# The first product's bank copied into a second bank of PSUM, and the second product accumulated there

## The chip, the cores and the metric

The kernel runs on one core of a Trainium2 chip. The metric is the device time of one execution, in microseconds. The engines are TensorE (PE in the profile; its weight loads are PEld), VectorE (DVE), ScalarE (ACT), GpSimd (POOL) and SyncE (SP). SP and POOL issue most DMAs here.

## The reference

One encoder layer on two sequences, a sample of 1024 tokens and a prompt of 512, with width 2048, in float32. What matters of it:

```python
h = rms_norm(x, norm_g)
z = h @ w_in                                   # 2048 -> 5632 columns
c_val, c_glu, c_gate, q, k, v, a_gate = jnp.split(z, split_points, axis=-1)
...                                            # rope on q and k
conv_out = conformer_conv(c_val, c_glu, ...) * jax.nn.silu(c_gate)   # 31 taps, layer norm, silu, @ w_pw
attn_out = banded_sink_attention(q, k, v, sink) * jax.nn.silu(a_gate)
mix = jnp.concatenate([conv_out, attn_out], axis=-1) @ w_out
return rms_norm(x + mix, final_norm_g)
```

## The kernel before

Every large product is made of matmuls of 128x128 weights against 512 tokens. For accuracy an operand is split into a high and a low part of a rounded format (`parts`, line 506: a ScalarE copy for the high part, a VectorE subtraction for the low one), and three matmuls stand for one: high by high, high by low, low by high.

The sample's input projection is written as *units* (class `Unit`). A unit multiplies two column tiles of the weights by two halves of the tokens over two groups of four row tiles. That is a product of 2x2 block matrices, and it is done in Winograd's form with seven block products instead of eight: P1, P2, P6, P5, P7, P3, P4 (the order `ALONE`, one name per step). Each is 4 x 3 = 12 matmuls, 84 for a unit. `SUMS` says which sum of tokens a product streams, `OPERAND` which split weight tile (`hl`, four per unit, made by `make0` to `make3`) it reads, `BANK` which of the unit's three PSUM banks it goes to. Products named in `FRESH` begin a bank, the others accumulate on what stands in it.

After each product `tap` takes the bank away. A ScalarE copy (line 236) goes to a buffer of the pools u or g, four buffers each, which are handed out in turn by `E()`. Where a partial result needs two banks, a VectorE addition follows (line 257). So the first result is: P1 copied, then P2's bank added to the copy; the bank of P1 goes on collecting P6, P7 and P4. `finish` hands a result on: in the first and third stage POOL's queue stores it (line 268), in the second and fourth a DMA of POOL's queue adds the stored half to it (line 501), and after four further steps (`landing`) its follow-up runs: gates, rope, silu.

The weights: `load0` and `load1` fetch two raw tiles of 512 KB by SP's queue into three buffers, `make0` splits the first, `make1` subtracts (three VectorE operations, line 143), then splits the sums, `less2` and `make2` follow on the second tile, `make3` on the last sum. There are three `hl` buffers; a product that is the last to read one gives it back, and `w_prep` is called in each product to make the next ones. A `Prep` says how many loads ahead are to be issued after it (`lead`).

The order of stages: a first plain unit, then seven units (first half of the rows, convolution columns), eight (second half of the same), fourteen (first half, the other columns) and fourteen (second half). At the head of the first, second and fourth the units run as a pair, product by product in turn. `switch` prepares the sums of tokens for the next stage in the last unit of the first and third. Beside the units, lanes of small work run by credit: the convolution's taps on VectorE, sums and norms, attention. After the units come the prompt's jobs, the pointwise products, the output projection in units of class `Onto`, and the last products for the prompt.

The Tile framework orders the instructions of each engine by priority and by its own reckoning of when each can begin, and sets the semaphores. `high_priority` moves an instruction ahead, `issue_after` behind another of the same engine. On the chip each engine takes its instructions in that order.

Of the kernel before, what the change touches and what calls it, by code (L numbers as in the profile page):

```python
# [57 lines left out]
ALONE = ("P1", "P2", "P6", "P5", "P7", "P3", "P4")  # L58
DIRECT = ("P1", "P2", "P3")
ENDS = (ALONE, ("P1", "P2", "P6", "P5", "P7", "P3", "P4"))  # L60
TURNS = ("P1", "P2", "P5", "P6", "P7", "P3", "P4")


# [30 lines left out]
class Unit:  # L94
# [10 lines left out]
    def __init__(self, e, w, cols, k, part, done=None, keep=None):  # L105
        self.e, self.k, self.part, self.done, self.keep = e, k, part, done, keep
        self.total = done is not None
        self.w = [w[c][:, k : k + 2 * HALF, :] for c in cols]
        self.before, self.after, self.d = [], {}, {}
        self.side = False  # L110
        self.order = ALONE
        self.sums = None


    def preps(self):
        return [Prep(load, make, 3) for load, make in ((self.load0, self.make0), (self.load1, self.make1), (None, self.make2), (None, self.make3))]

    def raw(self):
        return self.side([2, HALF, P], F32) if self.side else self.e.raw_tile()

    def load0(self):
        self.r1 = self.e.raw_tile()
# [12 lines left out]
    def make0(self):  # L135
        t = self.e.hl_tile()
        self.e.parts(t[:, 0], t[:, 1], self.r1)
        if self.keep:
            self.e.store(self.keep[0][:, self.k : self.k + 2 * HALF, :], t[:, 1].bitcast(F32).rearrange("p a b c -> p (a b) c"))
        return t  # L140

    def sub(self, out, x, y):
        self.e.nc.vector.tensor_tensor(out, x, y, ALU.subtract)

    def make1(self):

        if self.late:
            t2 = self.e.G([HALF, P]) if self.side or not self.total else self.e.A([HALF, P], F32)
        else:
            t2 = self.e.PT("p", NP, [HALF, P])  # L150
        r1, r2 = self.r1, self.r2
        self.sub(r1[:, 0], r2[:, 0], r1[:, 0])
        self.sub(t2, r2[:, 1], r1[:, 0])
        self.sub(r1[:, 1], r1[:, 1], t2)
        if self.sums:
            for name, x in (("P5", r1[:, 0]), ("P6", t2), ("P4", r1[:, 1])):
                self.e.store(self.sums[name], x)
        t = self.e.hl_tile()
        for o, x in enumerate((r1[:, 0], t2)):
            self.e.parts(t[:, 0, o], t[:, 1, o], x)  # L160
        return t

    def less2(self):
# [29 lines left out]
    def product(self, step, late):  # L193
# [4 lines left out]
        e.w_prep(i + 1)  # L198
        hl = e.hl[i]
        n = BANK[name]  # L200
        if name in FRESH:
            self.bank[n] = e.PS(self.tags[n], [W])
        acc = self.bank[n]
        toks = e.T[SUMS[name]]
        for j in range(HALF):
            for q, (l, r) in enumerate(((0, 0), (0, 1), (1, 0))):
                nc.tensor.matmul(  # L207
                    acc,
                    hl[:, l, o, j, :],
                    toks[j][:, r],  # L210
                    start=name in FRESH and j == 0 and q == 0,
                    stop=name in LAST and j == HALF - 1 and q == 2,
                    skip_group_check=True,
                )
            if j == 0:
                for fn in late:
                    fn()
                if step or not self.alone:
                    e.w_prep(i + self.look)
                else:  # L220
                    e.lessen(self)
                e.turn_over()
            e.tick(3 * MM)
        if step in (1, 3, 5, 6):
            e.hl.pop(i)
        for fn in self.after.get(step, ()):
            fn()
# [2 lines left out]
    def tap(self, name):  # L230

        e, nc = self.e, self.e.nc
        bank = self.bank[BANK[name]]
        if name not in ("P2", "P3"):
            t = e.E()
            nc.scalar.activation(t, bank, AF.Copy)  # L236
            self.copied = nc.cur_bb.bb.instructions[-1]
# [12 lines left out]
        elif name == "P3":  # L250
            self.add((0, 1), bank)
        else:
            self.d[1, 0] = t
            self.finish((1, 0))

    def add(self, n, x):
        self.e.nc.vector.tensor_tensor(self.d[n], x, self.d[n], ALU.add)
# [13 lines left out]
class Onto(Unit):  # L271
# [5 lines left out]

    def __init__(self, e, w, cols, k, source, part, done=None):
        super().__init__(e, w, cols, k, part, done)
        self.source, self.next, self.ahead = source, None, 2  # L280

    def begin(self, n):
# [96 lines left out]
class Prep:  # L379


    def __init__(self, load, make, lead=2, behind=False):
        self.load, self.make, self.lead, self.behind = load, make, lead, behind


class Job:
# [44 lines left out]
class Encoder:  # L431
# [199 lines left out]

    def w_prep_now(self, upto):
        while self.ready < min(upto, len(self.preps)):
            self.w_load(self.ready + 1)
            prep = self.preps[self.ready]
            with self.behind() if prep.behind else ExitStack():
                self.hl[self.ready] = prep.make()
            self.ready += 1
# [1236 lines left out]
def encoder(ctx, tc, a):  # L1875
# [18 lines left out]
    def grouped(units, two):  # L1894
        if not two:
            return [[u] for u in units]
        units[1].side = two
        return [units[:2]] + [[u] for u in units[2:]]

    items = [grouped(units, room) for units, room in zip([stages[0][1:]] + stages[1:], (e.A, e.F, None, e.F))]  # L1900
# [48 lines left out]
    def switch(unit, nxt, g, seq):  # L1949

        held = {}

        roomy = seq is sample

        def load(step):
            held[step] = seq.load_sum(SUMS[ALONE[step]], g, step % 3 or roomy and step == 6)

        def follow(step):
            for j, x in enumerate(held.pop(step)):
                seq.token_sum(SUMS[ALONE[step]], g, j, x)  # L1960
            if step < 4 - roomy:
                load(step + 3)
            elif step == 4 and roomy:
# [214 lines left out]
```

## Time and profile before

| | |
|---|---|
| median of three runs | 2076.07 us (2073.94 to 2077.29) |
| the profiled execution | 2079.13 us, span 2077.4 us |
| mean granted TensorE clock | 0.998 |
| PE busy | 2060.1 us, 9256 matmuls |
| VectorE busy | 1728.4 us |
| ScalarE busy | 1081.8 us |
| POOL busy | 157.9 us |
| HBM | 237 GB/s over the span |

The span runs from the first to the last instruction of one execution. Busy times are per engine and overlap. A row of the timeline has the start, the length, the engine, the line of the kernel, the operation with what it writes and reads, the count, and in brackets how long the engine stood idle before it and what ended that. A merged row of matmuls reaches from the first one's start to the last one's modelled end.

### The profile page before, as it was taken

The numbers are of one execution on the slowest core, as the hardware profiler recorded it, in microseconds if no ns is written. First come the engines' busy times: TensorE is split into PE (matmuls) and PEld (weight loads), VectorE is DVE, ScalarE is ACT, GpSimd is POOL, SyncE is SP. The second block draws the span as 40 slices with busy tenths as digits, with TensorE's granted clock in tenths as the row PEclk, the third lists the DMA queues.
The fourth block names the chain that finished last, engine by engine and source line by source line (L and its number), as shares of the span: only waits on it lengthen the run. The fifth ranks groups of instructions, "written<-read, shape, count | busy, mean of one in ns | idle before, by whom it ended". The sixth has DMA issues, their size and how long they took to land.

```text
span 2077.4 us, 27223 instructions
## 1 busy us (share of the span) xinstructions
PE 2060.1 (99%) x9256; PEld 1697.9 (82%) x9256; DVE 1728.4 (83%) x2843; ACT 1081.8 (52%) x1771; POOL 157.9 (8%) x240
## 2 busy tenths in 40 slices
PE   9999999999999999999999999999999999999998
PEld 8888888888888888788888888888888887888886
DVE  8768899998899899889766777776799978998877
ACT  7486445333465555655555777336553343454454
POOL 0111111111112111100000000000000111100000
PEclk9999999999999999999999999999999999999999
DMA  8888886864577777954555555997789898778897
GB/s 285 309 300 256 200 215 226 286 218 158 190 243 197 181 167 179 279 167 158 164 183 185 178 172 188 316 329 233 239 295 295 279 324 283 213 259 277 293 324 279
DMA packets 242300, 494.56 MB, mean 238 GB/s; under 512 B 23664, under 2 KB 84464, under 8 KB 242160
## 3 DMA queue, kind: packets, MB, share of 16 engines
q1 hardware_dynamic: 216352, 428.83, 62.1%
q0 software_dynamic: 24512, 61.88, 12.5%
q10 hardware_dynamic: 1296, 2.11, 0.3%
q8 instruction: 72, 1.18, 0.2%
q14 instruction: 68, 0.56, 0.1%
HBM read 331.77 MB, written 160.96 MB: 237 GB/s over the span
## 4 chain that ended last, share of the span: by engine, by line
PE 73%; issue 8%; DMA 8%; DVE 7%; ACT 2%; POOL 1%; SPq 0%; ACTq 0%; POOLq 0%; DVEq 0%
PE a L207 21%; PE a L670 13%; PE c L207 10%; PE b L670 6%; PE c L670 6%; PE b L207 5%; PE s L1169 2%; PE pv L1198 2%; PE a L1852 2%; PE s L207 2%; DVE hl L511 2%; PE pt L1203 1%; PE s L1852 1%; DVE t L511 1%; DMA p<-y_d 1%
## 5 line engine op out<-in xcount | busy, mean ns | idle before, releaser
L207 PE MATMUL a<-t,hl 128*128 128x512 f32 x2640 | 632.5, 390 | 1.8 <-ACT u L236 1.3
L207 PEld LDWEIGHTS a<-t,hl 128*128 128x128 f32 x2640 | 493.5, 188 | 108.4 <-ACT u L236 2.4
L511 DVE TENSOR_TENSOR hl<-raw,hl 128x1024 fp32r<-128x1024 f32 (+3 forms) x334 | 337.8, 1012 | 151.5 <-ACT hl L510 147.3
L510 ACT ACTIVATE hl<-raw 128x1024 fp32r<-128x1024 f32 (+3 forms) x334 | 296.8, 889 | 314.4 <-PE c L207 88.1
L670 PE MATMUL a<-t,hl 128*128 128x512 f32 x1344 | 326.3, 393 | 0.0
L207 PE MATMUL c<-t,hl 128*128 128x512 f32 x1320 | 319.1, 389 | 0.0
L670 PEld LDWEIGHTS a<-t,hl 128*128 128x128 f32 x1344 | 248.8, 188 | 50.4
L207 PEld LDWEIGHTS c<-t,hl 128*128 128x128 f32 x1320 | 247.4, 188 | 51.5 <-DVE u L304 0.2
L1041 DVE SCALAR_TENSOR_TENSOR f<-f,c_w_dw,f 128x512 f32<-128x512 f32 x248 | 172.9, 744 | 0.2
L670 PE MATMUL b<-t,hl 128*128 128x512 f32 x672 | 162.9, 392 | 1.5 <-DVE t L515 0.8
L670 PE MATMUL c<-t,hl 128*128 128x512 f32 x672 | 163.9, 393 | 0.0
L1004 DVE SCALAR_TENSOR_TENSOR f<-f,c_w_dw,f 128x512 f32<-128x512 f32 x232 | 163.4, 742 | 0.2
L207 PE MATMUL b<-t,hl 128*128 128x512 f32 x660 | 159.8, 389 | 0.0
L670 PEld LDWEIGHTS b<-t,hl 128*128 128x128 f32 x672 | 124.8, 188 | 27.5 <-DVE t L515 1.1
L670 PEld LDWEIGHTS c<-t,hl 128*128 128x128 f32 x672 | 124.6, 188 | 24.8
L207 PEld LDWEIGHTS b<-t,hl 128*128 128x128 f32 x660 | 123.7, 188 | 25.6
L1033 DVE SCALAR_TENSOR_TENSOR f<-f,w_both,f 128x512 f32<-128x512 f32 x120 | 89.8, 748 | 2.0
L236 ACT ACTIVATE u<-a 128x512 f32<-128x512 f32 x82 | 48.8, 595 | 77.3 <-PE a L207 70.6
L236 ACT ACTIVATE g<-a 128x512 f32<-128x512 f32 x78 | 46.5, 596 | 78.5 <-PE a L207 68.5
L1183 ACT ACTIVATE p<-p,tiny 128x384 f32<-128x384 f32 (+1 forms) x96 | 54.6, 570 | 45.9 <-DVE tiny L1180 36.2
L510 ACT ACTIVATE a<-pt 128x512 fp32r<-128x512 f32 x64 | 38.0, 593 | 64.6 <-PE pt L1203 64.4
L285 POOL DMA_DIRECT2D g<-xT_s x16 | 8.8, 551 | 743.1 <-DMA att_d<-u 669.0
(356 smaller groups left out, 2765.2 us busy)
## 6 DMA issues: line engine op xcount, KB each, us to landing
raw<-w_in SPq DMA_DIRECT2D x170, 512.0 KB, 5.2
raw<-w_out SPq DMA_DIRECT2D x31, 512.0 KB, 5.1
raw<-w_pw SPq DMA_DIRECT2D x24, 512.0 KB, 4.2
wsum_P<-raw SPq DMA_DIRECT2D x47, 256.0 KB, 3.6
raw<-wsum_P SPq DMA_DIRECT2D x18, 512.0 KB, 5.1
f<-x_s SPq DMA_DIRECT2D x16, 512.0 KB, 8.5
g<-wsum_P SPq DMA_DIRECT2D x28, 256.0 KB, 4.6
a<-sum_S SPq DMA_DIRECT2D x24, 256.0 KB, 6.1
```

Source lines behind the costliest of these rows:

```text
L207: nc.tensor.matmul(acc, hl[:, l, o, j, :], toks[j][:, r], start=name in FRESH and j == 0 and q == 0, stop=name in LAST and j == HALF - 1 a ...
L236: nc.scalar.activation(t, bank, AF.Copy)
L510: nc.scalar.activation(hi, x, AF.Copy)
L511: nc.vector.tensor_tensor(lo, x, hi.bitcast(F32), ALU.subtract)
L670: nc.tensor.matmul(job.acc[0], hl[:, l, kk // HALF, kk % HALF, :], r, start=i == 0 and p == 0, stop=i == nk - 1 and p == 2,)
L1004: nc.vector.scalar_tensor_tensor(t, h[:, j : j + T], w(j), t, ALU.mult, ALU.add)
L1033: nc.vector.scalar_tensor_tensor(m0, odd[:, j : j + H], both(j), m0, ALU.mult, ALU.add)
L1041: nc.vector.scalar_tensor_tensor(out, d[:, j : j + H], w(2 * j + k), out if j else m0, ALU.mult, ALU.add)
L1169: nc.tensor.matmul(ps[:, 0:n], qs[:, x, h], k[y][:, keys], start=p == 0, stop=p == 2)
L1183: nc.scalar.activation(p[:, 0:n], p[:, 0:n], AF.Exp, bias=nm[:, h : h + 1], accum_out=l[:, h : h + 1])
L1198: nc.tensor.matmul(pv, v[x][:, vs], pt[:, y], start=i == 0 and p == 0, stop=i == last and p == 2)
L1852: nc.tensor.matmul(acc[t], self.toks[name, m][:, x, i, t * P : (t + 1) * P], parts[i][l].rearrange("p a b -> p (a b)"), start=fresh and fi ...
```

## The change

For the units that run alone, the seven products are done in another order, `FORKED`: P1, P5, P6, P2, P7, P3, P4. P1 and P5 begin a bank. After P1, ScalarE copies its bank into the unit's second bank (`fork`) in place of a buffer; P2, now the fourth step, accumulates on that copy; after P2, ScalarE copies the second bank to a buffer, and that is the first result. The VectorE addition after P2 is gone. P5's copy is taken two steps earlier and waits for P7 as before.

The three subtractions of `make1` become a function of their own, `less1`; where they were in `make1` they now stand at the end of `make0`, save in the `Onto` units. `make0` therefore needs the second raw tile too: `Prep` has a new number `needs`, the loads that must be issued before the tile is made (three for the first, one for the others). A split tile is given back when no later product of the order reads it. `switch` takes the order of its unit. The pairs at the heads of stages and the `Onto` units call `together`, which gives them the old order and the old tap.

```diff
--- before.py
+++ after.py
@@ -58,6 +58,7 @@
 ALONE = ("P1", "P2", "P6", "P5", "P7", "P3", "P4")
 DIRECT = ("P1", "P2", "P3")
 ENDS = (ALONE, ("P1", "P2", "P6", "P5", "P7", "P3", "P4"))
+FORKED = ("P1", "P5", "P6", "P2", "P7", "P3", "P4")
 TURNS = ("P1", "P2", "P5", "P6", "P7", "P3", "P4")
 
 
@@ -108,15 +109,22 @@
         self.w = [w[c][:, k : k + 2 * HALF, :] for c in cols]
         self.before, self.after, self.d = [], {}, {}
         self.side = False
-        self.order = ALONE
+        self.order, self.fresh = FORKED, ("P1", "P5")
         self.sums = None
 
 
     def preps(self):
-        return [Prep(load, make, 3) for load, make in ((self.load0, self.make0), (self.load1, self.make1), (None, self.make2), (None, self.make3))]
+        early = 1 if self.late else 3
+        return [
+            Prep(load, make, 3, needs=needs)
+            for load, make, needs in ((self.load0, self.make0, early), (self.load1, self.make1, 1), (None, self.make2, 1), (None, self.make3, 1))
+        ]
 
     def raw(self):
         return self.side([2, HALF, P], F32) if self.side else self.e.raw_tile()
+
+    def together(self):
+        self.order, self.fresh = ALONE, FRESH
 
     def load0(self):
         self.r1 = self.e.raw_tile()
@@ -137,12 +145,14 @@
         self.e.parts(t[:, 0], t[:, 1], self.r1)
         if self.keep:
             self.e.store(self.keep[0][:, self.k : self.k + 2 * HALF, :], t[:, 1].bitcast(F32).rearrange("p a b c -> p (a b) c"))
+        if not self.late:
+            self.less1()
         return t
 
     def sub(self, out, x, y):
         self.e.nc.vector.tensor_tensor(out, x, y, ALU.subtract)
 
-    def make1(self):
+    def less1(self):
 
         if self.late:
             t2 = self.e.G([HALF, P]) if self.side or not self.total else self.e.A([HALF, P], F32)
@@ -152,12 +162,18 @@
         self.sub(r1[:, 0], r2[:, 0], r1[:, 0])
         self.sub(t2, r2[:, 1], r1[:, 0])
         self.sub(r1[:, 1], r1[:, 1], t2)
+        self.t2 = t2
         if self.sums:
             for name, x in (("P5", r1[:, 0]), ("P6", t2), ("P4", r1[:, 1])):
                 self.e.store(self.sums[name], x)
+
+    def make1(self):
+        if self.late:
+            self.less1()
         t = self.e.hl_tile()
-        for o, x in enumerate((r1[:, 0], t2)):
+        for o, x in enumerate((self.r1[:, 0], self.t2)):
             self.e.parts(t[:, 0, o], t[:, 1, o], x)
+        self.t2 = None
         return t
 
     def less2(self):
@@ -198,7 +214,7 @@
         e.w_prep(i + 1)
         hl = e.hl[i]
         n = BANK[name]
-        if name in FRESH:
+        if name in self.fresh:
             self.bank[n] = e.PS(self.tags[n], [W])
         acc = self.bank[n]
         toks = e.T[SUMS[name]]
@@ -208,7 +224,7 @@
                     acc,
                     hl[:, l, o, j, :],
                     toks[j][:, r],
-                    start=name in FRESH and j == 0 and q == 0,
+                    start=name in self.fresh and j == 0 and q == 0,
                     stop=name in LAST and j == HALF - 1 and q == 2,
                     skip_group_check=True,
                 )
@@ -221,7 +237,7 @@
                     e.lessen(self)
                 e.turn_over()
             e.tick(3 * MM)
-        if step in (1, 3, 5, 6):
+        if all(OPERAND[n][0] != p for n in self.order[step + 1 :]):
             e.hl.pop(i)
         for fn in self.after.get(step, ()):
             fn()
@@ -231,6 +247,8 @@
 
         e, nc = self.e, self.e.nc
         bank = self.bank[BANK[name]]
+        if self.order is FORKED and name in ("P1", "P2"):
+            return self.fork(name, bank)
         if name not in ("P2", "P3"):
             t = e.E()
             nc.scalar.activation(t, bank, AF.Copy)
@@ -253,6 +271,18 @@
             self.d[1, 0] = t
             self.finish((1, 0))
 
+    def fork(self, name, bank):
+
+        e = self.e
+        t = e.PS(self.tags[1], [W]) if name == "P1" else e.E()
+        e.nc.scalar.activation(t, bank, AF.Copy)
+        if name == "P1":
+            self.bank[1] = t
+            self.copied = e.nc.cur_bb.bb.instructions[-1]
+        else:
+            self.d[0, 0] = t
+            self.finish((0, 0))
+
     def add(self, n, x):
         self.e.nc.vector.tensor_tensor(self.d[n], x, self.d[n], ALU.add)
         self.finish(n)
@@ -277,6 +307,7 @@
 
     def __init__(self, e, w, cols, k, source, part, done=None):
         super().__init__(e, w, cols, k, part, done)
+        self.together()
         self.source, self.next, self.ahead = source, None, 2
 
     def begin(self, n):
@@ -379,8 +410,8 @@
 class Prep:
 
 
-    def __init__(self, load, make, lead=2, behind=False):
-        self.load, self.make, self.lead, self.behind = load, make, lead, behind
+    def __init__(self, load, make, lead=2, behind=False, needs=1):
+        self.load, self.make, self.lead, self.behind, self.needs = load, make, lead, behind, needs
 
 
 class Job:
@@ -631,8 +662,8 @@
 
     def w_prep_now(self, upto):
         while self.ready < min(upto, len(self.preps)):
-            self.w_load(self.ready + 1)
             prep = self.preps[self.ready]
+            self.w_load(self.ready + prep.needs)
             with self.behind() if prep.behind else ExitStack():
                 self.hl[self.ready] = prep.make()
             self.ready += 1
@@ -1895,6 +1926,8 @@
         if not two:
             return [[u] for u in units]
         units[1].side = two
+        for u in units[:2]:
+            u.together()
         return [units[:2]] + [[u] for u in units[2:]]
 
     items = [grouped(units, room) for units, room in zip([stages[0][1:]] + stages[1:], (e.A, e.F, None, e.F))]
@@ -1949,15 +1982,16 @@
     def switch(unit, nxt, g, seq):
 
         held = {}
+        order = unit.order
 
         roomy = seq is sample
 
         def load(step):
-            held[step] = seq.load_sum(SUMS[ALONE[step]], g, step % 3 or roomy and step == 6)
+            held[step] = seq.load_sum(SUMS[order[step]], g, step % 3 or roomy and step == 6)
 
         def follow(step):
             for j, x in enumerate(held.pop(step)):
-                seq.token_sum(SUMS[ALONE[step]], g, j, x)
+                seq.token_sum(SUMS[order[step]], g, j, x)
             if step < 4 - roomy:
                 load(step + 3)
             elif step == 4 and roomy:
```

## The prediction

> **What bounds the kernel now.** I read the head of the page first, then the busy time by stretch, then the timeline of single steps, and last the rows in which the matrix engine (PE) waits.
>
> ```profile
> span 2077.4 us, 27223 instructions
> PE 2060.1 (99%) x9256; PEld 1697.9 (82%) x9256; DVE 1728.4 (83%) x2843; ACT 1081.8 (52%) x1771; POOL 157.9 (8%) x240
> PE 73%; issue 8%; DMA 8%; DVE 7%; ACT 2%; POOL 1%; SPq 0%; ACTq 0%; POOLq 0%; DVEq 0%
> ...
> 170.00:500.00 330.00, 330.00 (x1458) 273.19 (x1457) 295.68 (x458) 141.70 (x219) 48.02 (x69) 1.00 0.75 221
> 610.00:860.00 250.00, 248.94 (x1101) 204.15 (x1100) 229.14 (x344) 141.49 (x221) 47.07 (x54) 1.00 0.77 193
> ...
> 30.04:856.03 825.99, 822.48 (x3612) 676.84 (x3611) 1.00 0.76 225
> ```
>
> The reader is to see that PE is busy for 99% of the span and heads the chain of waits with 73%. In the stretches the columns are length, then busy time of PE, weight loads, VectorE, ScalarE and POOL. From 170 to 500 us PE has no idle time at all while VectorE is at 295.68 of 330.00, that is 90%. The last row holds only the matmuls of line 207, those of the units: the first to the last of them span 825.99 us, and there are 3612. The changed order applies only here.
>
> Busy does not say that PE is at its pace, so the steps themselves come next. One unit of the third stage, steps P1 (the last 12 matmuls of the row before 474.15), P2, P6, P5, P7, P3 and P4:
>
> ```profile
> 471.63 0.60 ACT L236 ACTIVATE g<-a 128x512 f32<-128x512 f32 x1 [1.52 <-PE a L207]
> 474.15 2.88 PE L207 MATMUL b<-t,hl 128*128 128x512 f32 x12
> 474.35 0.60 ACT L236 ACTIVATE u<-a 128x512 f32<-128x512 f32 x1 [2.12 <-PE a L207]
> 476.87 2.88 PE L207 MATMUL a<-t,hl 128*128 128x512 f32 x12
> 477.44 0.68 DVE L257 TENSOR_TENSOR u<-b,u 128x512 f32<-128x512 f32 x1
> 479.59 2.88 PE L207 MATMUL c<-t,hl 128*128 128x512 f32 x12
> 482.31 2.88 PE L207 MATMUL a<-t,hl 128*128 128x512 f32 x12
> 485.03 2.88 PE L207 MATMUL c<-t,hl 128*128 128x512 f32 x12
> 487.75 4.01 PE L207 MATMUL a<-t,hl 128*128 128x512 f32 x17
> 488.00 0.63 ACT L510 ACTIVATE hl<-raw 128x512 fp32r<-128x512 f32 x1 [2.17 <-PE c L207]
> 489.56 0.69 DVE L511 TENSOR_TENSOR hl<-raw,hl 128x512 fp32r<-128x512 f32 x1
> 490.17 0.68 DVE L511 TENSOR_TENSOR hl<-p,hl 128x512 fp32r<-128x512 f32 x1
> ```
>
> Steps start every 2.72 us (474.15, 476.87, 479.59, 482.31 and so on): 12 matmuls at 0.2267 us. A unit of seven steps takes 19.04 us. All 3612 at that pace are 818.7 us. The window has 825.99, so only 7.3 us of it are stalls or other matmuls. This is the ceiling of any gain inside the units, 0.35% of the whole, whatever is taken off another engine.
>
> **What changes, and what each part costs.** Which units: the pairs at the head of the first, second and fourth stages keep the old order (so do the Onto units of the output projection). That leaves 5 + 6 + 14 + 12 = 37 units. The matmuls are the same in number, so PE's own work does not change.
>
> *The addition and the copies.* Rows of the listing by form:
>
> ```profile
> L236 ACT ACTIVATE u<-a 128x512 f32<-128x512 f32 x82 | 48.8, 595 | 77.3 <-PE a L207 70.6 <-DMA sum_S<-u 3.6 <-issue 2.5
> L257 DVE TENSOR_TENSOR u<-b,u 128x512 f32<-128x512 f32 x20 | 13.6, 682 | 0.0
> L510 ACT ACTIVATE hl<-raw 128x512 fp32r<-128x512 f32 x118 | 74.3, 630 | 151.4 <-PE c L207 62.4 <-DVE raw L143 34.6 <-PE b L207 25.1
> L143 DVE TENSOR_TENSOR raw<-raw,raw 128x512 f32<-128x512 f32 x55 | 37.7, 685 | 0.7 <-DMA raw<-w_in 0.4
> ```
>
> Each unit loses one VectorE addition (0.682 us, 37 times: 25.2 us) and gains one ScalarE copy out of PSUM (0.595 us, 22.0 us). P1's copy stays but now lands in PSUM. No row shows that. Its nearest rows are PSUM to SBUF at 0.595 and SBUF to SBUF at 0.630 us; a gain or a loss of 0.1 us either way isn't excluded, and I take 0.60, the row that shares its source. On the path it counts for nothing: in the steady unit the copy is done at 474.95 and the step that accumulates on its bank, P6, begins at 476.87. In the new order P6 stands in the same third place. The cover is 1.9 us; if it went, each us of delay would cost 37 us. P2, now fourth, has a whole step more. VectorE's 25.2 us were hidden behind PE (90% busy beside PE without a gap), so by the ceiling above they give back at most what stalls now.
>
> The Trainium skill, "ScalarE: Activation LUTs", section "ACT is a hardware spline evaluator", says that a ScalarE write to PSUM is the lower-latency one, and gives 186 ns plus 0.833 ns an element, an estimate of 0.61 us for 512. The trace agrees on the PSUM-to-SBUF form (0.595); no run here shows the PSUM target. By that rule the 22.0 us on ScalarE would shrink by little, and the sum stays, since they lie beside PE.
>
> *Buffers.* P1 no longer takes a buffer of the u and g pools, P2 takes one two steps later and P5's is held for three steps in place of one. The number per unit is five before and after. P2's DMA on POOL's queue moves two or three steps later; the four of a unit then stand one step of 2.72 us apart, and POOL is busy for 19% of that stretch (47.07 of 250.00). Nothing is added to SP's queue, but the second raw weight tile has to be issued before the first is split. I cost that at nothing, as the look-ahead already issues it there; without that cover VectorE would stand behind a load.
>
> *The order of weights.* P5 comes second, so the operand sums (less1, three VectorE subtractions of 0.685 us, 2.06 us in all) move ahead into the first split, two steps earlier, and the second split must be ready at the second product, not the third. In the steady unit its first half, which P5 reads, is done at 490.25, and the next unit's second product starts at 493.19: 2.9 us to spare. P5 reads only that half; the other is for P6. In the fourth stage it is different:
>
> ```profile
> 646.42 2.88 PE L207 MATMUL b<-t,hl 128*128 128x512 f32 x12
> 647.80 0.68 DVE L511 TENSOR_TENSOR hl<-raw,hl 128x512 fp32r<-128x512 f32 x1
> 815.74 0.63 ACT L1067 ACTIVATE g<-u 64x512 f32<-64x512 f32 x1 [3.07 <-DMA u<-part_q]
> 820.03 2.88 PE L207 MATMUL b<-t,hl 128*128 128x512 f32 x12
> 820.06 0.69 DVE L511 TENSOR_TENSOR hl<-raw,hl 128x512 fp32r<-128x512 f32 x1
> ```
>
> Here the half is done at 648.48 and 820.75, after the second product has begun (646.42, 820.03). P5 reads the low part first in its third matmul, 0.45 us in, so at these times it would be late by 1.6 and 0.3 us. But what makes it late moves too. In the row at 815.74 ScalarE stands for 3.07 us behind the DMA that adds P2's partial result, ahead of the split. That is the follow-up of P2's result, emitted three steps after its addition: the sixth step, just before the split. With P2 fourth it is emitted at the first step of the next unit, behind the split. With the subtractions gone as well, I take no stall, and keep 0.3 to 1.6 us a unit for the range.
>
> *The first pair.* It keeps its order but gets the earlier sums:
>
> ```profile
> 31.59 1.21 DVE L511 TENSOR_TENSOR hl<-raw,hl 128x1024 fp32r<-128x1024 f32 x1
> 32.76 2.88 PE L207 MATMUL s<-t,hl 128*128 128x512 f32 x12
> ```
>
> The split ends at 32.80, where the product that reads it starts at 32.76. Three subtractions put ahead of it could cost up to 2.06 less the 0.45 us, 1.6 us; the first subtraction was ahead already and the weights may land after it. I take 0.3.
>
> *The stalls that are there.* What an earlier or freer engine could give back:
>
> ```profile
> 85.03 0.60 ACT L236 ACTIVATE u<-a 128x512 f32<-128x512 f32 x1 [3.63 <-DMA sum_S<-u]
> 85.68 5.78 PE L207 MATMUL a<-t,hl 128*128 128x512 f32 x24 [1.08 <-ACT u L236]
> 629.21 0.60 ACT L236 ACTIVATE u<-a 128x512 f32<-128x512 f32 x1 [0.25 <-DMA gate_d<-u]
> 629.86 3.01 PE L207 MATMUL a<-t,hl 128*128 128x512 f32 x12 [0.22 <-ACT u L236]
> 842.30 3.01 PE L207 MATMUL a<-t,hl 128*128 128x512 f32 x12 [0.35 <-ACT g L236]
> 857.14 10.67 PE L670 MATMUL b<-t,hl 128*128 128x512 f32 x44 [0.49 <-DVE hl L511]
> 868.63 0.73 PE L670 MATMUL b<-t,hl 128*128 128x512 f32 x2 [0.82 <-DVE t L515]
> ```
>
> At 85 us P7's copy waits for a u buffer that a store still reads; it still takes one: 0. At 629 us P1's copy waits for a buffer that it won't need any more: -0.22. At 842 us P1's copy stands behind token splits on ScalarE: 0. At 857 us the first job waits for VectorE, which runs without a gap there and has one addition less: -0.49. At 868 us the wait is behind a load and a ScalarE split: 0.
>
> **The sum.** The profiled execution took 2079.13 us (span 2077.4). 0.3 - 0.22 - 0.49 = -0.4 us: 2078.7. The median of the runs shown is 2076.07, 3.06 lower than that execution, so on its scale 2075.7.
>
> **Rivals.** *Slower, by a late P5 operand.* Its place is the fourth stage, its price the lateness above: three units like the one at 646 us at 1.6 and nine like the one at 820 at 0.3 are 7.5 us, 2083.2 on the median's scale; all twelve at 1.6 would be 19 us. It decides once the low half ends on average 0.35 us past the third matmul of P5 (12 x 0.35 = 4.2, the 0.2%). For it speaks that ScalarE is in order and gets work; against it the move of P2's follow-up, and in the steady unit 2.9 us to spare. Chance 0.14.
>
> *Faster, by stalls that vanish.* All 7.3 us over the pace, 2076.07 - 7.3 = 2068.8 at the most: VectorE has 25 us more, and if each wait above ends sooner, and none comes, this is what is there to win. Against it: the longest stall (1.08) waits for a store, not for VectorE. It counts as faster only past 4.2 us, over half of the ceiling. Chance 0.11.
>
> *Faster, by a pace of PE that isn't its floor.* If VectorE's reads of PSUM slowed the matmuls, 37 x 84 = 3108 of them could run quicker with fewer reads. The rows speak against it: the step at 476.87 us, with an addition beside it, takes the same 2.72 us as that at 479.59 us without one. A gain of 0.011 us each would be 34 us, 2042. Chance 0.02.
>
> The 0.011 is the difference to the rule of the Trainium skill, "TensorE: Matmul & The Clock Gate", section "Part 1: The HAM clock gate (the "warmup" mystery)": 215.7 ns for a warm matmul of 512 columns. The trace has 226.7 throughout at a clock of 1.00; no run here shows 215.7.
>
> *The change does nothing measurable*, since a copy replaces an addition on two engines that both have cover: that is my forecast, 0.73, with its own range 2072 to 2079.
>
> The bound between change and no change is 0.2%, 4.2 us, about what a measurement of this kernel can tell. Faster is 0.11 + 0.02 = 0.13, slower 0.14, same 0.73. The range runs from 2070.5, inside the vanishing stalls, to 2082, into the late operand.
>
> **What would show it.** Right: 37 fewer additions on line 257 and PE's units still 2.72 us a step; the span of line 207's matmuls 825 to 826 us; ScalarE some 22 us busier, VectorE some 25 less; the P1 copy within 1 us after its product. Wrong: PE or weight-load rows in P5's place that wait for the split (VectorE, line 511) or for ScalarE; P6 waiting for the copy into the second bank; VectorE waiting for a raw weight load at the subtractions; or a step other than 2.72 us. Stalls that appear past 870 us, where no code changes, would be the order of the work shifting, which I can't price.

## The result, and the profile after

Slower, by half a per cent: 2087.11 us median of four runs (2082.65 to 2088.49) against 2076.68 (2073.94 to 2077.9); ratio 1.0047, 95% interval 1.0034 to 1.0059. I had forecast 2075.7 and a range up to 2082. The ratios here and below are worked out from executions in the usual state and are not the quotients of the medians, and one execution of fourth_only_p, of 7392.66 us, is not in its ratio.

The profiled execution of the changed kernel took 2085.75 us. The head of its page, and the windows that answer to those shown of before (its units begin at 29.70 and the first job at 865.45):

```profile
span 2084.0 us, 27272 instructions
PE 2060.4 (99%) x9256; PEld 1698.0 (81%) x9256; DVE 1706.9 (82%) x2806; ACT 1100.8 (53%) x1808; POOL 157.6 (8%) x240
...
170.00:500.00 330.00, 329.06 (x1450) 271.49 (x1449) 286.37 (x442) 151.15 (x238) 48.72 (x71) 1.00 0.74 224
...
29.70:865.45 835.75, 825.87 (x3612) 677.68 (x3611) 1.00 0.73 222
```

PE's work is the same. The 3612 matmuls of the units take 835.75 us where they took 825.99: 9.8 us more. From there to the end of the span it is 2.8 us less (2084.0 - 865.45 = 1218.6, against 2077.4 - 856.03 = 1221.4). So in these two executions all of the loss lies in the units. (Their spans differ by 6.6 us, the medians by 10.4; what follows accounts for this pair of executions.) From 170 to 500 us, where PE had no idle time, 0.94 us are missing now; VectorE is at 286.37 there, from 295.68.

The steps themselves are as they were. One unit of the third stage, PE and then the copies out of PSUM (line 278 is the new copy, 254 the old one):

```profile
479.50 2.88 PE L223 MATMUL c<-t,hl 128*128 128x512 f32 x12
482.22 2.88 PE L223 MATMUL a<-t,hl 128*128 128x512 f32 x12
484.94 2.88 PE L223 MATMUL b<-t,hl 128*128 128x512 f32 x12
...
479.76 0.58 ACT L278 ACTIVATE b<-a 128x512 f32<-128x512 f32 x1 [2.18 <-PE a L223]
482.42 0.60 ACT L254 ACTIVATE u<-c 128x512 f32<-128x512 f32 x1 [1.11 <-PE c L223]
485.68 0.58 ACT L254 ACTIVATE g<-a 128x512 f32<-128x512 f32 x1
487.86 0.60 ACT L278 ACTIVATE u<-b 128x512 f32<-128x512 f32 x1 [1.60 <-PE b L223]
490.58 0.60 ACT L254 ACTIVATE g<-a 128x512 f32<-128x512 f32 x1 [1.17 <-PE a L223]
```

Still 2.72 us a step. P1's copy into the second bank ends at 480.34 and P2, which accumulates there, begins at 484.94. But the last four rows are four buffers of the pools u and g, taken in four steps in a row (after P5, P6, P2 and P7). In the kernel before it was three, and P1's (at 474.35 in the prediction's rows) stood apart:

```profile
479.79 0.60 ACT L236 ACTIVATE g<-a 128x512 f32<-128x512 f32 x1 [2.04 <-PE a L207]
482.51 0.60 ACT L236 ACTIVATE u<-c 128x512 f32<-128x512 f32 x1 [2.12 <-PE c L207]
...
485.23 0.60 ACT L236 ACTIVATE g<-a 128x512 f32<-128x512 f32 x1 [1.17 <-PE a L207]
```

The largest waits of PE in the changed kernel; the numbers are the sum in us, how often, and the longest:

```profile
PE b L223 <- DVE t L546: 3.4, 2, 2.6
PE a L223 <- ACT g L254: 2.6, 3, 2.1
PE b L701 <- ACT t L545: 1.6, 1, 1.6
PE s L773 <- DVE u L768: 1.4, 1, 1.4
```

Before, the longest wait inside the units was 1.08 us. Here are the places. At 103 us, in the first stage:

```profile
100.36 0.69 DVE L826 TENSOR_TENSOR g<-f 128x512 f32<-128x512 f32 x1 [1.59 <-DMA sum_S<-g]
...
102.10 0.75 DVE L824 SCALAR_TENSOR_TENSOR u<-f,norm_n,g 128x512 f32<-128x512 f32 x1
...
102.88 1.59 SPq L535 DMA_DIRECT2D sum_S<-u  x2
...
104.30 0.60 ACT L278 ACTIVATE u<-b 128x512 f32<-128x512 f32 x1 [5.12 <-DMA sum_S<-u]
...
104.92 0.60 ACT L254 ACTIVATE g<-a 128x512 f32<-128x512 f32 x1
...
105.57 5.74 PE L223 MATMUL a<-t,hl 128*128 128x512 f32 x17 [2.06 <-ACT g L254]
```

```profile
102.00:105.57 3.57, 1.51 (x7) 0.93 (x5) 3.57 (x7) 1.24 (x3) 0.27 (x1) 0.99 0.80 307
105.57:110.40 4.83, 4.83 (x14) 3.90 (x15) 2.76 (x5) 2.24 (x5) 1.35 (x3) 0.65 0.91 231
```

The lane that prepares sums (lines 822 to 826) writes a u buffer, which SP stores. By the rows P2's copy is given that buffer next, and ScalarE stands 5.12 us until the store has landed; P7's copy comes behind it, and P4, which adds to P7's bank, waits. The store is only the end of this wait: it began at 99.18, and VectorE had written the buffer only at 102.85, after it had itself stood 1.59 us for a store (the first row) and had made a weight split. The second fence has windows (length, busy PE, weight loads, VectorE, ScalarE and POOL, granted clock): after the wait the clock was 0.65 for 4.83 us. In the last row ahead of them 17 matmuls take 5.74 us; at 0.2267 us they are 4.0 with the modelled end. So this stall cost 2.06 + 1.7, close to 4 us.

At 599 us, at the head of the fourth stage:

```profile
588.67 0.69 DVE L153 TENSOR_TENSOR raw<-raw,raw 128x512 f32<-128x512 f32 x1 [1.64 <-DMA raw<-w_in]
...
594.81 0.68 DVE L153 TENSOR_TENSOR raw<-f,raw 128x512 f32<-128x512 f32 x1
...
600.95 2.07 DVE L546 SCALAR_TENSOR_TENSOR t<-p,c_norm_g,t 128x512 fp32r<-128x512 f32 x3
...
601.75 2.14 PE L223 MATMUL b<-t,hl 128*128 128x512 f32 x8 [2.64 <-DVE t L546]
```

The pair there works in the old order and needs P2's token sums (A12) second. But `switch` prepares them in the order of the unit in which it runs, and there P2 is now fourth; they come behind the pair's own subtractions (line 153). The first of these had stood 1.64 us for its raw weight tile. It is the same at 177 us, where PE waits 0.80 us and a subtraction before it stood 2.21 us for its tile. At 152 us the spreading of norms (line 773) waits 1.36 us for VectorE, against 0.16 before; why VectorE comes later there is not shown. A smaller wait of the first kind is at 784.61: P7's copy stands 2.82 us for a store of its buffer, and PE waits 0.43.

Together the four large places are 2.06 + 1.7 + 2.64 + 0.80 + 1.36 = 8.6 us; the wait of 1.08 us at 85 us is gone. That is 7.5 of the 9.8 us. The rest is not all waiting. Of the 9.8 us, 3.4 are the same 3612 matmuls taking longer (825.87 us against 822.48), and the slow clock at 103 us is 1.7 of them. The waits that are left are under half a us each. Part of the longer matmuls lies right behind the waits: in the prediction's rows twelve take 3.01 us behind the wait at 629 us, where twelve without a wait take 2.88. I did not place these one by one.

### The profile page after: what moved, and what is told of

Same layout as the page of the kernel before. It is cut to its first block, busy times and chain, and to the rows that moved or that the text cites. A ratio compares the mean times of both kernels' runs of the same rounds, so it can differ in the third digit from the quotient of the medians.

```text
span 2084.0 us, 27272 instructions
## 1 busy us (share of the span) xinstructions
PE 2060.4 (99%) x9256; PEld 1698.0 (81%) x9256; DVE 1706.9 (82%) x2806; ACT 1100.8 (53%) x1808; POOL 157.6 (8%) x240
## 4 chain that ended last, share of the span: by engine, by line
PE 83%; DVE 7%; DMA 5%; issue 3%; ACT 1%; POOL 0%; SPq 0%; ACTq 0%; POOLq 0%; DVEq 0%
PE a L223 23%; PE a L701 14%; PE c L223 12%; PE b L701 6%; PE c L701 6%; PE b L223 5%; PE s L1200 2%; PE s L1883 2%; PE pv L1229 2%; PE a L1883 2%; PE s L223 2%; DVE hl L542 2%; PE pt L1234 1%; PE pt L223 1%; DVE f L1035 1%
## 5 line engine op out<-in xcount | busy, mean ns | idle before, releaser
L542 DVE TENSOR_TENSOR a<-pt,a 128x512 fp32r<-128x512 f32 x64 | 44.1, 689 | 26.4 <-ACT a L541 25.6
L449 ACT ACTIVATE hl<-raw 128x1024 fp32r<-128x1024 f32 x43 | 45.4, 1057 | 33.2 <-PE a L701 13.4
```

Of the source, the lines that this page charges most:

```text
L449: e.nc.scalar.activation(t[:, 0], raw, AF.Copy)
L542: nc.vector.tensor_tensor(lo, x, hi.bitcast(F32), ALU.subtract)
```

## The experiments

Ratios are to the kernel before, run beside each version on the same chip, with the 95% interval. The times are medians.

| | units in the new order | us | before, us | ratio |
|---|---|---|---|---|
| after_again, the changed kernel | 37 | 2086.48 | 2076.43 | 1.0058 [1.0042, 1.0073] |
| order_only | 37 | 2093.91 | 2076.48 | 1.0080 [1.0068, 1.0092] |
| copy_only | 37, products in the old order | 2086.54 | 2076.62 | 1.0047 [1.0031, 1.0063] |
| sums_early | 0 | 2075.51 | 2076.62 | 0.9994 [0.9984, 1.0005] |
| switch_old | 35 | 2084.73 | 2076.48 | 1.0037 [1.0024, 1.0051] |
| p_buffer | 37 | 2092.64 | 2076.48 | 1.0077 [1.0064, 1.0090] |
| switch_p_buffer | 35 | 2084.28 | 2076.48 | 1.0036 [1.0024, 1.0048] |
| ends_old | 34 | 2085.87 | 2076.62 | 1.0040 [1.0027, 1.0053] |
| ends_first_old | 30 | 2080.92 | 2076.62 | 1.0018 [1.0007, 1.0030] |
| middle_only | 19 | 2075.82 | 2076.43 | 0.9997 [0.9989, 1.0006] |
| fourth_only | 11 | 2079.50 | 2076.43 | 1.0010 [1.0001, 1.0019] |
| first_only | 4 | 2080.33 | 2077.65 | 1.0010 [0.9999, 1.0021] |
| first_only_p | 4 | 2077.88 | 2077.65 | 1.0002 [0.9992, 1.0011] |
| fourth_only_p | 11 | 2081.38 | 2077.65 | 1.0014 [1.0003, 1.0025] |
| vector_copy | 37 | 2089.77 | 2076.43 | 1.0058 [1.0042, 1.0073] |

**The parts of the change.** First the new order and the early subtractions, with the old copy and the VectorE addition:

```diff
-        self.order, self.fresh = FORKED, ("P1", "P5")
+        self.order, self.fresh = FORKED, FRESH
...
-        if self.order is FORKED and name in ("P1", "P2"):
-            return self.fork(name, bank)
```

> The new order of products and the early subtractions stay; P1's copy goes to a buffer again, P2 begins its own bank and is added on VectorE. Theory 'buffers' (P2's copy on ScalarE waits for a u or g buffer whose store has not landed, and P7's copy stands behind it): that wait is gone, so the time falls by some 4 us from the changed kernel to about 6 us over the kernel before. Theory 'pair' (the sums of A12 come too late for the pair at the head of a stage): those 4 us stay. Theory 'late split': all 10 us over the kernel before stay. If the copy into PSUM itself were the cost: the time of the kernel before.

None of these theories came true. The version is 7 us slower than the changed kernel: with this order the new copy is a gain, and the order with the early subtractions costs 17 us. Its two largest waits in 30 to 900 us:

```profile
PE s L771 <- DVE u L766: 3.6, 2, 3.4
PE b L699 <- ACT t L543: 3.3, 1, 3.3
```

The first is the spreading of norms, the second is in the first job. A copy's wait for a buffer is there too, at 96 us: PE waits 2.38 us for it. Then the copy without the order, P2 adding on it right behind P1:

```diff
-FORKED = ("P1", "P5", "P6", "P2", "P7", "P3", "P4")
+FORKED = tuple(list(ALONE))
...
+        if self.order is FORKED and name == "P2":
+            for fn in late:
+                fn()
+            late = []
```

> The changed kernel with its products in the old order: P2 follows P1 and must wait for the copy into its bank (0.2 us after P1, 0.58 us long). 37 units at some 0.85 us each: 31 us over the kernel before, if the copy's place on the path is what the new order is for. If PE could start ahead of it: none of this.

The wait in every unit did not come. The framework put four matmuls of another product (bank c) between P1 and P2. The first fence has these rows and then the place of its largest wait, the second its waits for the copy into the second bank:

```profile
480.34 1.07 PE L227 MATMUL c<-t,hl 128*128 128x512 f32 x4
480.60 0.58 ACT L282 ACTIVATE b<-a 128x512 f32<-128x512 f32 x1 [2.18 <-PE a L227]
481.25 3.00 PE L227 MATMUL b<-t,hl 128*128 128x512 f32 x12
...
103.71 0.60 ACT L258 ACTIVATE u<-c 128x512 f32<-128x512 f32 x1 [3.67 <-DMA sum_S<-u]
...
104.36 2.22 PE L227 MATMUL c<-t,hl 128*128 128x512 f32 x7 [2.53 <-ACT u L258]
```

```profile
PE b L227 <- ACT b L282: 2.2, 2, 1.6
```

The largest wait, 2.53 us, is again at a buffer that is being stored. Here too P1 takes no buffer and P2 does. Twice, 2.2 us in all, P2 did wait for the copy. These are 4.7 us, where the median lost some 10; the rest I did not place. Last, the early subtractions alone, in the kernel before: `less1` at the end of `make0`, and `needs`.

> The kernel before with the early subtractions alone: less1 at the end of the first split and three loads ahead of it, the order and the addition as before. Theory 'late load' (VectorE stands behind a raw tile's load at the subtractions, 2.21 and 1.64 us in the changed kernel's profile ahead of the pairs): 1 to 3 us over the kernel before. Theory 'order': the subtractions are harmless, within 1 us of it.

No difference: with the old order the early subtractions and loads cost nothing. This does not clear them in the new order. In this run VectorE never stands more than 0.24 us for a raw tile in the units, while in the changed kernel it stood 2.21 and 1.64 us ahead of the pairs. In the control below, the second of these is 0.26 us and PE's wait behind it is still 1.92 us, so the late tile is not what makes most of that wait.

**The heads of the stages.** The last units of the first and third stages, in which `switch` runs, in the old order:

```diff
+    stages[0][-1].together()
+    stages[2][-1].together()
```

> The changed kernel, with the old order and the old addition in the last unit of the first and of the third stage alone, which prepares the next stage's token sums. Theory 'pair': the waits of 1.07 us at 177 us and 2.92 us at 599 us go, so some 4 us less than the changed kernel, about 6 us over the kernel before. Theory 'buffers': the wait at 103 us stays, and nothing else moves, about 10 us over.

The waits at 177 and 599 us are gone; the listing of waits has no row for line 546 in the units any more, and the largest that is left is for P7's copy:

```profile
PE a L223 <- ACT g L254: 3.1, 2, 2.6
```

So it is shown that these waits come from the new order in the unit ahead of the pair. The edit also puts that unit's own products and its tap back, so that it is the order of the sums and not these is read from line 546 in the rows and from the code. The time came back by 2 us, where the waits were 3.4 us, and the intervals overlap.

**The buffers.** P2's copy to a buffer of another pool, without and with the edit above:

```diff
-        t = e.PS(self.tags[1], [W]) if name == "P1" else e.E()
+        t = e.PS(self.tags[1], [W]) if name == "P1" else e.PT("p", NP, [W])
```

> The changed kernel, with P2's copy going to a buffer of the p pool in place of the u and g pools. Theory 'buffers': the waits at 103 us (4.3 us with the slow clock behind it) and before P4 at 784, 804 and 843 us (1.8 us) shrink or go, 4 to 6 us less than the changed kernel, about 4 to 6 us over the kernel before. Theory 'pair': unchanged, about 10 us over.

> Both of the last two edits. If 'buffers' and 'pair' together are the loss: within 2 us of the kernel before, at about 2077. If something else costs (the late split, a slower copy): 4 us over or more.

In p_buffer the wait at 104 us was 0.68, but at the head of the fourth stage a subtraction stood for a store of the new pool, and the pair behind it:

```profile
104.62 3.69 PE L223 MATMUL a<-t,hl 128*128 128x512 f32 x15 [0.68 <-ACT g L254]
...
599.42 0.69 DVE L153 TENSOR_TENSOR p<-f,raw 128x512 f32<-128x512 f32 x1 [3.45 <-DMA part_gate<-p]
...
602.76 1.65 PE L223 MATMUL b<-t,hl 128*128 128x512 f32 x3 [4.45 <-DVE t L546]
```

The shortage had moved to the other pool. With both edits that is avoided, and the time is that of switch_old. It is not the 2077 us that I expected if these two were the whole loss: nearly 8 us are left.

**Stage by stage.** Units put back to the old order with `together()`. First the last unit of the fourth stage as well, then the single units of the first stage too:

```diff
+    for stage in (0, 2, 3):
+        stages[stage][-1].together()
```

> The changed kernel, with the old order and the old addition in the last unit of the first, third and fourth stage. New theory 'junctions': the later second product costs where a unit meets other work, since it brings the sums of A12 late for the pair and puts P2's added half and its follow-up late, ahead of the first job's splits. Then the waits at 177, 599 and about 870 us go back to what they are in the kernel before, and some 4 us go, to about 6 us over it. Rival 'buffers alone': no fall, 10 us over.

```diff
+    for u in stages[0][3:] + [stages[2][-1], stages[3][-1]]:
+        u.together()
```

> The same, and all single units of the first stage in the old order too, so that 30 units keep the new one. Theory 'junctions and first stage' (in the first stage the copies of P2, P7 and the sums of tokens want the same u and g buffers): all the places of large waits are in the old order, so within 2 us of the kernel before, the rest being the waits of P4 in the fourth stage (1.8 us). Rival, a cost in every unit (ScalarE's extra copy, the late split): still 6 us over or more.

The fourth stage's last unit gave nothing, and the wait at the first job stayed (2.69 us), so my theory of the junctions fell there. The first stage's units gave 5 us (the intervals just touch), and with them the wait at 103 us went and the one at 152 us fell to 0.16. Then the inner units of the second and third stages alone, their complement in the fourth, and the changed kernel again as control:

```diff
+    for u in stages[0][3:] + [stages[2][-1]] + stages[3][2:]:
+        u.together()
```

> The new order and tap stay in 19 units alone: the six single units of the second stage and the first thirteen of the third. The single units of the first and fourth stages and the last of the third are as before. Theory (the loss is a few places where a copy stands behind a buffer still being stored, in the first and fourth stages, and the sums for the pairs): nothing of it is left, 2074 to 2079 us, ratio 0.999 to 1.001, and no unit stall above 0.8 us between 160 and 600 us. Rival (a little is lost in every unit, 4.3 us over the 30 units of the run with first stage and ends old): 19/30 of it, 2.7 us, so about 2079.5, ratio 1.0013. Rival (the junction to the first job and the fourth stage suffer from what the order did earlier): waits at 775 to 870 us stay and it is 2080 or more.

```diff
+    for u in stages[0][3:] + stages[1][2:] + stages[2] + stages[3][-1:]:
+        u.together()
```

> The complement: the new order and tap in eleven single units of the fourth stage alone, all others as before. Theory: the stalls between 775 and 876 us are there as in the run with first stage and ends old, about 4 us: 2079 to 2082 us, ratio 1.0012 to 1.0025, and none ahead of 600 us that the kernel before does not have. Rival (a cost in every unit): 11/30 of 4.3 us, 1.6 us, 2078.3. Rival (those stalls come from the order of the earlier stages): same as before, 2076.6.

> The changed kernel unaltered, as the control beside the other three on the same chip: 2083 to 2089 us, ratio 1.003 to 1.006 to the kernel before. A second profile tells which of its stalls are the same in two executions: by theory those at 103, 177, 599 and 784 us and at the junction near 875 us are, and if others take their place the list of places is chance while the sum is not.

PE's waits in 30 to 900 us of middle_only (two more are 0.2 each), and then the two largest of the control:

```profile
PE b L701 <- DVE t L546: 0.7, 1, 0.7
PE c L223 <- ACT u L254: 0.4, 1, 0.4
PE a L223 <- ACT u L254: 0.3, 1, 0.3
```

```profile
PE b L223 <- DVE t L546: 2.7, 2, 1.9
PE a L223 <- ACT g L254: 2.2, 1, 2.2
```

Nineteen units in the new order cost nothing (at most 1.0006, 1.2 us): there is no price per unit. In the control the same places wait as in the first profile, so they are not chance. The fourth stage costs 3 us in the median. Some 0.35 us of that is outside the span: its times exceed its spans by 2.05 to 2.16 us, those of the kernel before beside it by 1.72 to 1.82. Its profiled execution took 2076.75 us, hardly more than the kernel before, and can't show where the rest goes: it has 1.22 and 0.81 us at the first job, against 0.49 and 0.82 before. But one thing is to be seen there. With the middle stages in the new order too (ends_first_old), copies hold PE up at 776, 796 and 836 us, for 0.96, 0.63 and 1.39 us; in fourth_only none of these waits is there.

Does P2's copy hold P7's up because ScalarE works in order? It was given to VectorE:

```diff
+            e.nc.vector.tensor_copy(t, bank)
```

> P2's result is copied out of PSUM by VectorE in place of ScalarE; the rest is the changed kernel. P1's copy stays with ScalarE. Theory (P7's copy stands behind P2's on ScalarE, which is in order, while P2's waits for a buffer): the stall at about 103 us falls from 4.3 to under 1.5 us, those at 784 to 843 us fall by half, and the time by 3 to 5 us, to 2081 to 2084. Rival (the buffer itself is short, whoever copies): P7's copy waits for its own buffer, the stall at 103 us stays above 2 us and the time at 2085 to 2088. Rival (VectorE's order is what counts, as in the run with the new order and the old addition): VectorE stands at the buffer with the splits behind it, and the time is above 2089.

```profile
104.98 0.68 DVE L283 COPY u<-b 128x512 f32<-128x512 f32 x1
...
105.45 0.60 ACT L254 ACTIVATE g<-a 128x512 f32<-128x512 f32 x1 [5.66 <-DMA sum_S<-g]
...
106.10 2.29 PE L223 MATMUL a<-t,hl 128*128 128x512 f32 x6 [1.97 <-ACT g L254]
```

No. Freed of P2's copy, P7's copy waits for its own buffer, and PE as long as before (1.97 against 2.06). My theory of ScalarE's order fell. At this place the buffers are short, whoever copies. In time this kernel is not told apart from the control (2089.77 and 2086.48 us, with the same interval).

Last, the new order in the first stage's units alone, with u and g and with the pool p, and the fourth stage with p:

```diff
+    for u in stages[0][-1:] + stages[1][2:] + stages[2] + stages[3][2:]:
+        u.together()
```

> The new order and tap in four single units of the first stage alone (its last unit and all later stages as before). Theory: the stall near 103 us of some 4 us is there, that near 151 us of 1.5 us too, nothing else above the kernel before: 2080 to 2083 us, ratio 1.002 to 1.003. Rival (the parts are not additive; the first stage costs only where later stages are changed too): within 2 us of before.

> As the run with the new order in four units of the first stage, and P2's result goes to a buffer of the pool p in place of u or g, so that these pools are asked for four buffers a unit and not five. In the first stage alone nothing else is moved into the way of that pool at the heads of later stages. Theory (the u and g buffers, waiting for stores, are the cause in this stage): the wait for P7's copy near 103 us falls below 0.9 us and the time comes back by 2 to 4 us, to 2076.5 to 2079. Rival (the order of products is the cause, whatever buffers): the same as the run it is compared with, 2080 to 2083. Rival (the shortage moves to pool p inside the stage): VectorE waits for a store of a p buffer between 95 and 175 us, and the time is above 2082.

> As the run with the new order in eleven units of the fourth stage, with P2's result in pool p. That run was 3 us above the kernel before. Theory for this stage (the follow-ups of its last units run late and hold the splits for the first job behind them): the buffers are not the cause here, the wait at the first job near 867 us stays at 2 us or more and the time at 2078 to 2082. Rival (the buffers are the cause here too): back to 2075.5 to 2077.5. Rival (the shortage moves to pool p): above 2082.

In first_only the wait at 103 us is there (1.63 us) and the one at 152 us too (1.36); its 2.7 us are not clear of no change. With the pool p they are 0.2, as the buffers would have it, but the intervals overlap and the profile of that run does not show why: P7's copy still stood for a store there.

```profile
104.83 0.60 ACT L254 ACTIVATE g<-a 128x512 f32<-128x512 f32 x1 [4.98 <-DMA sum_S<-g]
...
105.48 1.89 PE L223 MATMUL a<-t,hl 128*128 128x512 f32 x7 [1.77 <-ACT g L254]
```

One buffer a unit less does not free the one that P7 is dealt next. In the fourth stage the pool made no difference, so its 3 us are not shown to be the buffers', and stay open. So does the sum: 2.7 and 3.1 us alone, nothing in the middle, but 9 to 10 together. The units of first_only, middle_only and fourth_only are just those of ends_old (4 + 19 + 11 = 34). Added up, their ratios are 1.0017; ends_old, without the heads' waits, has 1.0040 with a lower end of 1.0027. So the stages seem to delay one another, and the waits at 776 to 836 us are a place of it, but I did not separate how. Nor did any run keep the new order and move the lane of sums out of its way, which would test the buffers of the first stage directly. No version beat the kernel before by more than the noise.

## Why the prediction was wrong

The step that failed is the one on buffers: "The number per unit is five before and after." With that the takes had no term in the sum. The number was right, and it was the wrong thing to count. The takes moved to other steps, and buffers are handed out in turn, also to the lane of sums. At 103 us the one dealt next was not yet stored. The row at 85 us that I quoted (3.63 us for a store) was the warning. I put it at 0 because P7 still takes one. In the changed kernel that wait is gone (from 30 to 92 us PE is busy for 62.00 of 62.00), and there is one of the same kind at 103 us, of about 4 us with the low clock. That the new order of the first stage brings it is shown: PE waits there for P7's copy in the profiles of the changed kernel, of the control (2.21), of switch_old (2.62), of ends_old (2.13) and of first_only (1.63), and not in ends_first_old, middle_only and fourth_only, where the first stage has the old order (0.2 to 0.4 us for another copy are left near there). That a store holds the buffer is in the rows. Which change of the takes does it is not shown. Four takes in a row are not what it needs: in first_only_p P2 takes a p buffer, only two of the others follow one another, and the wait is 1.77 us.

The same paragraph says "I cost that at nothing" of the raw weight tile that has to be issued earlier, and names VectorE behind a load as a sign of being wrong. That sign came, ahead of the pairs at 177 and 599 us (2.21 and 1.64 us). What it costs there is not separated from the order of the sums.

A step was missing: that the pairs keep the old order, while the sums they start on are prepared in the new one. The diff of `switch` shows it. The waits at these places are 0.80 and 2.64 us, where I had nothing, and they went with switch_old.

These steps are not the whole loss. With the first stage and the units ahead of the pairs in the old order (ends_first_old) the kernel is still 4 us over the one before, and what costs these is open.

The rival on the slower side had the sign and not the mechanism. P5's operand was not late: in the changed kernel's profile no wait of PE in the units of over 0.02 us is for a weight split, and the 19 units of middle_only lose nothing. In fourth_only, where only the fourth stage has the new order, PE waits 0.40 us for a split once, at 628 us. My range ended at 2082, below the 2083.2 that I had worked out for this very rival.

The small terms. The 0.3 us for the first pair did not show in the changed kernel's profile; six of the other profiled runs have 0.19 to 0.30 us there, at 33 us. The waits of 0.22 at 629 and 0.49 at 857 us went as forecast, and others took their place at the first job, where the splits stand behind silu (line 1014) on ScalarE: 1.65 and 0.34 us, against 0.49 and 0.82 before.

```profile
873.43 1.06 ACT L449 ACTIVATE hl<-raw 128x1024 fp32r<-128x1024 f32 x1 [0.40 <-ACT u L1014]
...
876.10 0.50 PE L701 MATMUL b<-t,hl 128*128 128x512 f32 x1 [1.65 <-ACT t L545]
...
877.41 2.11 PE L701 MATMUL b<-t,hl 128*128 128x512 f32 x8 [0.34 <-DVE t L546]
```

The 2.72 us a step and P1's cover (its copy begins 0.26 us after the next product) came as written. The ceiling on gains was not put to the test. The span of the units' matmuls, for which I had written 825 to 826 us, did not: it is 835.75.

The copies and the addition were right in number: 37 fewer VectorE instructions and 37 more of ScalarE. VectorE is 21.5 us less busy, not 25.2, and ScalarE 19.0 busier, not 22.0. The copy into PSUM is a little shorter than I took it:

```profile
L278 ACT ACTIVATE b<-a x37: 576/582/582, 70.7 to 849.3; 128x512 f32<-128x512 f32 x37
L278 ACT ACTIVATE g<-b x19: 574/599/600, 78.9 to 857.7; 128x512 f32<-128x512 f32 x19
```

The columns are the shortest, the median and the longest in ns. 0.582 against 0.599 us: inside the 0.1 that I allowed, and of no effect on the sum.

The forecast of "no change" was too sure. With PE at 99% a change of order has little to win but the 7.3 us over the pace, and hardly any slack to hide the waits that it makes. The ceiling that I had put on the gain had no counterpart for the loss.

## What to carry to other kernels

When an order changes, do not only count buffers but list at which step each is taken and given back, and who else draws from the same pool; a take that moves can meet a store that was out of its way. Look for code that prepares data in one unit's order for another that keeps the old one. Where the bounding engine has no slack, price a reordering with losses that are as large as the waits already seen for the same resource, and try it stage by stage: here it cost nothing in the inner units of two stages.

## What the runs showed of the hardware

A wait of about 2 us of PE can cost nearly twice that. After the 2.06 us wait at 105.57 the granted clock was 0.65 over the next 4.83 us; in the control a wait of 2.21 us at the same place left it at 1.00:

```profile
105.60:110.40 4.80, 4.71 (x21) 3.91 (x22) 3.36 (x6) 3.77 (x9) 1.97 (x4) 1.00 0.96 281
```

The Trainium skill, "TensorE: Matmul & The Clock Gate", section "What's actually happening", has the clock fall to half after an idle window of about 3.4 us and says that the window runs freely. That two equal waits end differently agrees with a free window. That a wait of 2.06 us was enough does not agree with the stated length, and here the measurement decides. The length alone does not settle it: in the control the wait of 1.92 us at 599 us was followed by a clock of 0.83 from 600 to 610 us, while the 2.64 us at the same place in the first profile left it at 1.00. The runs do not show what decides.
